# An encoder kernel on one core: the dt step cut into four pieces, the gates' products in 512 columns, the norm's second half on VectorE

## The chip, the core and the metric

One core of a Trainium2 chip runs the kernel. Five engines work on their own queues and wait for each other by semaphores: TensorE (PE, with its weight loads shown as PEld), VectorE (DVE), ScalarE (ACT), GpSimd (POOL) and SyncE (SP, which only issues transfers here). The metric is the device time of one execution in microseconds (us).

## The reference, cut to what matters

Two layers, 512 tokens of width 1024, all in float32. Each layer is

```
h    = rms_norm(x, norm1_w)
z, xbc, dt_raw, q, k, v = split(h @ w_in)
xs, B, C = split(silu(conv7(xbc)))
dt   = softplus(dt_raw + dt_bias)                  # two directions x 16 heads
y    = ssd(xs, dt, -exp(a_log), B, C) forward + backward + d_skip * xs
y    = rms_norm(y * silu(z))                       # per group of 512
attn = windowed_gqa(q, k, v, sink, bias)
x    = x + concat(y, attn) @ w_out
h    = rms_norm(x, norm2_w);  g, u = split(h @ w_up)
x    = x + (silu(conv3(g)) * u) @ w_down
```

and a final norm. The state-space part (ssd) works in chunks of 128 tokens: it needs the running sums of `a*dt` inside a chunk, their exponentials, and a decay matrix per head, `exp(sum_l - sum_s)`.

## The kernel before, in words

Tokens lie in four tiles of 128 (`NT`), the width in eight k-tiles. Every dense product is made of three matmuls (`mm3`, L277 to L280): each operand is split into a rounded part and a rest, and hi·hi, hi·lo and lo·hi are summed in PSUM. Weights come in units of 128 x 1024 by SP's DMA into three raw buffers; ACT rounds a unit (`whi`, L161), DVE makes the rest (`wlo`, L162), into three split buffers. `take` (L114) hands out a unit and issues the split of the unit three further on ahead of other work. PSUM has eight banks: four dense ones (`pd`, from `psd`) and four small ones (`psm`, from `pss`).

A scheduler sets the order of the instructions on each engine after `start.close()` (L538), from the order in the code and its own idea of when things are ready, so that a statement's place in the code isn't its place on an engine. Pools, buffer counts and priorities bind it.

The stages of a layer, in order: the value and dt columns (`vdt`); `dt_step` (L544), which makes softplus of dt in a chain of small DVE operations (`sp_e`, `sp_w`, `sp_a`), the running sums by six matmuls with triangular matrices (L581), their exponentials `ex` (L582), a logarithm of dt (`own`, L585 to L596), and turns the running sums `run` so that their transposes can go to DRAM (`sums`, L602), from where they are fetched as broadcast rows later; then the k columns; then ten dense pieces (list `dense`, L981), with attention's steps run in between (`Side`, L400); then the gates `g_z` (L832), with the steps of ssd group 0 in between: `fetch` (rows from DRAM), `decay` (L906 to L911: four additions and four exponentials on ACT, a predicated copy and a product `em` on DVE), `inner` (L922), `outer` (L937 to L945), and at the end a `turn` per token tile (L950); then the out projection `g_out` with ssd group 1 in between; `o2` and the norm; the FFN; `dn` and the next norm.

A gate unit is 4 k-tiles by 256 columns. A half of a group's columns takes two units, held together, and its four token tiles go in pairs: a pair fills one dense bank (2 x 256 columns, 48 matmuls), ACT takes Silu of the bank (L848), and ssd steps follow. Silu, Exp/Ln and the rest need different tables in ACT; the tables are loaded by ACT_TABLE_LOAD instructions in front of the operations that need them.

`norm_token` (L320) squares a token tile on ACT, finds the factor on POOL (L332, L333), and scales and weights both halves: the first by one DVE instruction (L342), the second by ACT (L344) and then POOL (L345). `turn_split` (L309) turns a half by four transposes, and ACT and DVE split it. It runs in three places: after `o2` of each layer and after `dn` of layer 0.

Of the kernel before, what the change touches and what calls it, by code (L numbers as in the profile page):

```python
# [7 lines left out]
F32 = mybir.dt.float32  # L8
# [38 lines left out]
def encoder_kernel(  # L47
# [122 lines left out]
    for i in range(DEPTH):  # L170
# [17 lines left out]
        for g in range(GROUPS):  # L188
            for half in range(2):
                pair(f"z{g}{half}", [(512 * g + 256 * half, 256)])  # L190
# [129 lines left out]
    def norm_token(npool, t, wb, dst):  # L320
# [13 lines left out]
        for b, cs in enumerate(halves):  # L334
            if dst is None:
                if b == 0:
                    S.mul(xn[:, cs], xn[:, cs], rs)
                else:
                    V.scalar_tensor_tensor(xn[:, cs], x_sb[t][:, cs], rs, wb[:, cs], ALU.mult, ALU.mult)
                nc.sync.dma_start(out[t * P : (t + 1) * P, cs], xn[:, cs])  # L340
            elif b == 0:
                V.scalar_tensor_tensor(xn[:, cs], x_sb[t][:, cs], rs, wb[:, cs], ALU.mult, ALU.mult)  # L342
            else:
                S.mul(xn[:, cs], x_sb[t][:, cs], rs)  # L344
                G.tensor_tensor(xn[:, cs], xn[:, cs], wb[:, cs], ALU.mult)  # L345
        if dst is None:
            return
        for b in range(2):
            turn_split(xn, t, b, dst)
# [120 lines left out]
    for i in range(DEPTH):  # L470
        side = Side()
        with ExitStack() as mix:
# [17 lines left out]
            dtx = ExitStack()  # L490
            dtp = dtx.enter_context(pool(f"dt_{i}", bufs=1, reuse_waits="tile"))
            run = dtp.tile([P, NT, 2, 16], F32, name=nm("run"))
            xdt = dtp.tile([P, NT, 32], F32, name=nm("xdt"))
# [49 lines left out]

            def dt_step():  # L544

                def et(name, shape, dt=F32):
                    return dtp.tile([P] + shape, dt, name=nm(name))

                sp_e = et("sp_e", [NT, 32])
                sp_w = et("sp_w", [NT, 32])  # L550
                sp_w2 = et("sp_w2", [NT, 32])
                sp_a = et("sp_a", [NT, 32])
# [7 lines left out]
                for n in (15, 13, 11, 9, 7, 5, 3):  # L560
# [4 lines left out]


                adt = sp_e
                V.scalar_tensor_tensor(
                    adt,
# [5 lines left out]
                )  # L575
                ps = small_bank()
                cum = ps[:, : 6 * 64].rearrange("p (n c h) -> p n c h", n=6, c=NT)
                for n, (m, o) in enumerate(
                    ((f(t_le), 0), (f(t_gt), 0), (f(t_ge), 16), (f(t_lt), 16), (ones, 0), (ones, 16))
                ):  # L580
                    mm(cum[:, n], m, adt[:, :, o : o + 16], start=True, stop=True)  # L581
                S.activation(ex, cum, AF.Exp)  # L582

# [6 lines left out]

                for d in range(2):
                    S.copy(run[:, :, d], cum[:, 2 * d])
# [4 lines left out]
                psr = small_bank()  # L597
                for c in range(NT):
                    turn128(psr[:32, c * P : (c + 1) * P], run[:, c].rearrange("p d h -> p (d h)"), ident)
                runT = dtp.tile([32, NT, P], F32, name=nm("runT"))  # L600
                V.tensor_copy(runT, psr[:32].rearrange("p (c l) -> p c l", c=NT))
                nc.gpsimd.dma_start(sums[i].rearrange("c r l -> r c l"), runT)  # L602
                V.tensor_tensor(sd[:, 0], ex[:, 1], dts[:, :, 0:16], ALU.mult)
                V.tensor_tensor(sd[:, 1], ex[:, 3], dts[:, :, 16:32], ALU.mult)
# [6 lines left out]
            dtx.close()  # L611
# [147 lines left out]
            def xbc(g, r):  # L759
# [16 lines left out]
                def bc_turn():  # L776
# [14 lines left out]
                    for c in range(NT):  # L791
                        sl = slice(c * P, (c + 1) * P)
                        junk = ep.tile([P, P], F32, tag="junk", name=nm("junk"), bufs=2)
# [38 lines left out]
            def g_z(g, r):  # L832
                sz = act_tile(F32)
                r["sz"] = sz
                for half in range(2):
                    ws = [take((i, f"z{g}{half}", j)) for j in range(2)]
                    cs = slice(256 * half, 256 * half + 256)
                    for tp in range(2):
                        bank = dense_bank()
                        for t in (2 * tp, 2 * tp + 1):  # L840
                            o = bank[:, (t % 2) * 256 : (t % 2) * 256 + 256]
                            sl = slice(t * P, (t + 1) * P)
                            for kt in range(KT):
                                hv, lv = (w.rearrange("p (k c) -> p k c", k=4)[:, kt % 4] for w in ws[kt // 4])
                                ah, al = hT[kt // 4]
                                mm3(o, ah[:, kt % 4, sl], al[:, kt % 4, sl], hv, lv, kt == 0, kt == KT - 1)
                        flush()
                        S.activation(sz[:, 2 * tp : 2 * tp + 2, cs], bank.rearrange("p (t c) -> p t c", t=2), AF.Silu)  # L848
                        yield
# [3 lines left out]
            def ssd_steps(sp, g, r):  # L853
# [123 lines left out]
                return [lambda k=k: step(k) for k in range(-1, 10)] + [lambda c=c: turn(c) for c in range(NT)]  # L977
# [3 lines left out]
            dense = [xs0[0], g_q(0), xs0[1], g_q(1), xs0[2], g_q(2), xs1[0], g_q(3), xs1[1], xs1[2]]  # L981
            for n, gen in enumerate(dense):
                side.run(gen, RATE_A if n > 1 else 0)
                if n == 7:
# [7 lines left out]
            side.steps += ssd_steps(sp, 0, r0)  # L992
# [10 lines left out]
            side.steps += ssd_steps(sp, 1, r1)  # L1003
# [151 lines left out]
```

## Time and profile before

| | |
|---|---|
| median of 3 runs | 1551.32 us (1548.27 to 1552.07) |
| the profiled execution | 1550.66 us, its span 1549.0 us |
| mean granted clock of TensorE | 0.994 of full speed |
| busy: PE, PEld, DVE | 1508.9, 1238.0, 876.5 us |
| busy: ACT, POOL | 793.4, 174.7 us |
| transfers | 161.48 MB, 104 GB/s over the span |

The span is the profiled stretch on the core; the execution's time also holds 1.66 us around it. PE is busy in nearly all of it, so the time is what PE has to do and the few places where it stands. Matmuls overlap, so an instruction's duration is longer than the distance to the next one: for sums, the distance between starts is used. Layer 0 begins at 0 us, layer 1 at 780 us; the gates of layer 0 run from 232 us to 306 us.

### The profile page before, as it was taken

How to read it: one execution, taken by the hardware profiler on the slowest of the kernel's cores; microseconds unless marked ns; L12 is line 12 of the kernel's file. 1: busy time of each engine (PE TensorE's matmuls, PEld its weight loads, DVE VectorE, ACT ScalarE, POOL GpSimd, SP SyncE). 2: the span in 40 equal slices, each digit the busy share in tenths (PEclk: the TensorE clock that was granted, in tenths of full speed). 3: DMA queues.
4: the chain of work that ended last, by engine and by line, in shares of the span. 5: the costliest groups of instructions: out<-in, count | busy, mean ns of one | idle time of the engine just before them, and what ended most of it. 6: DMA issues, size and time to landing. Idle time of an engine off the chain costs nothing.

```text
span 1549.0 us, 20219 instructions
## 1 busy us (share of the span) xinstructions
PE 1508.9 (97%) x7680; PEld 1238.0 (80%) x7680; DVE 876.5 (57%) x1406; ACT 793.4 (51%) x1464; POOL 174.7 (11%) x246
## 2 busy tenths in 40 slices
PE   7999999999999999999999999999999999999997
PEld 5787778877788888888887777887778888888886
DVE  5676777776644444433367777777666434443333
ACT  4467988863543233322356779788435323332223
POOL 2000002423200000000010000053232000000002
PEclk9899999999999999999999999999999999999999
DMA  6532333453323333322343322355422333333231
GB/s 206 156 82 76 83 85 103 134 169 95 108 88 98 102 95 96 95 96 95 99 137 104 89 75 62 83 123 182 132 95 82 95 97 101 101 96 96 95 96 68
DMA packets 113080, 161.48 MB, mean 104 GB/s; under 512 B 7932, under 2 KB 90108, under 8 KB 112975
## 3 DMA queue, kind: packets, MB, share of 16 engines
q1 hardware_dynamic: 104756, 132.60, 27.7%
q0 software_dynamic: 7648, 27.50, 6.7%
q8 instruction: 60, 0.98, 0.3%
q14 instruction: 38, 0.30, 0.1%
q10 hardware_dynamic: 578, 0.10, 0.0%
HBM read 155.82 MB, written 8.55 MB: 106 GB/s over the span
## 4 chain that ended last, share of the span: by engine, by line
PE 86%; ACT 4%; DVE 3%; issue 3%; POOL 2%; DMA 2%; POOLq 0%; ACTq 0%; DVEq 0%
PE pd L280 22%; PE pd L278 22%; PE pd L279 22%; PE psm L278 3%; PE psm L279 3%; PE psm L280 3%; PE psm L690 2%; PE psm L680 2%; PE psm L922 1%; PE psm L646 1%; DMA rows<-sums 1%; PE psm L647 1%; PE psm L937 1%; ACT whi L161 1%; PE psm L314 1%
## 5 line engine op out<-in xcount | busy, mean ns | idle before, releaser
L278 PE MATMUL pd<-t,whi 128*128 128x512 f32 (+1 forms) x1088 | 419.5, 386 | 1.5 <-ACT whi L161 1.5
L280 PE MATMUL pd<-t,wlo 128*128 128x512 f32 (+1 forms) x1088 | 419.4, 386 | 0.4 <-DVE wlo L162 0.4
L279 PE MATMUL pd<-t,whi 128*128 128x512 f32 (+1 forms) x1088 | 418.9, 385 | 0.0
L162 DVE TENSOR_TENSOR wlo<-raw,whi 128x1024 fp32r<-128x1024 f32 (+1 forms) x214 | 260.5, 1221 | 241.3 <-ACT whi L161 241.0
L161 ACT CAST whi<-raw 128x1024 fp32r<-128x1024 f32 (+1 forms) x214 | 221.8, 1040 | 240.9 <-PE pd L279 213.6
L278 PEld LDWEIGHTS pd<-t,whi 128*128 128x128 f32 x1088 | 204.7, 188 | 40.8 <-ACT whi L161 1.7
L280 PEld LDWEIGHTS pd<-t,wlo 128*128 128x128 f32 x1088 | 204.7, 188 | 40.2 <-issue 1.5
L279 PEld LDWEIGHTS pd<-t,whi 128*128 128x128 f32 x1088 | 205.0, 188 | 38.3 <-issue 0.8
L278 PE MATMUL pd<-whi,t 128*128 128x256 f32 (+2 forms) x544 | 188.9, 347 | 0.0
L279 PE MATMUL pd<-wlo,t 128*128 128x256 f32 (+2 forms) x544 | 180.3, 331 | 4.0 <-DVE wlo L162 3.9
L280 PE MATMUL pd<-whi,t 128*128 128x256 f32 (+2 forms) x544 | 181.7, 334 | 0.7 <-DVE t L962 0.7
L279 PEld LDWEIGHTS pd<-wlo,t 128*128 128x128 f32 x544 | 103.9, 191 | 17.2 <-DVE wlo L162 4.6
L278 PEld LDWEIGHTS pd<-whi,t 128*128 128x128 f32 x544 | 103.9, 191 | 13.7 <-issue 3.8
L280 PEld LDWEIGHTS pd<-whi,t 128*128 128x128 f32 x544 | 103.8, 191 | 11.5 <-DVE t L962 1.6
L1097 ACT CAST ph<-t 128x512 fp32r<-128x512 f32 x40 | 24.9, 623 | 143.0 <-PE psm L279 132.5
L1098 DVE TENSOR_TENSOR pl<-t,ph 128x512 fp32r<-128x512 f32 x40 | 27.7, 692 | 114.8 <-ACT ph L1097 114.8
L395 DVE SCALAR_TENSOR_TENSOR sg<-pd,fprm,sg 128x511 f32<-128x511 f32 x88 | 65.9, 748 | 30.7 <-ACT sg L389 29.0
L648 DVE CUSTOM_DVE_ANT_0 s<-psm,bias,sink_all 128x256 f32<-128x256 f32 (+1 forms) x128 | 65.6, 547 | 21.2 <-PE psm L647 8.0
L662 ACT ACTIVATE s<-s,nm 128x257 f32<-128x257 f32 (+1 forms) x128 | 70.5, 554 | 3.3 <-DVE nm L659 3.1
L395 DVE SCALAR_TENSOR_TENSOR xT<-pd,cprm,xT 128x511 f32<-128x511 f32 (+2 forms) x96 | 66.6, 742 | 5.2 <-PE psm L680 4.3
L278 PE MATMUL pd<-whi,ph 128*128 128x512 f32 x176 | 68.9, 391 | 0.0
L279 PE MATMUL pd<-wlo,ph 128*128 128x512 f32 x176 | 68.7, 390 | 0.0
(205 smaller groups left out, 2181.1 us busy)
## 6 DMA issues: line engine op xcount, KB each, us to landing
raw<-in_w_up_dram SPq DMA_DIRECT2D x88, 512.0 KB
raw<-in_w_in_dram SPq DMA_DIRECT2D x52, 512.0 KB
raw<-in_w_down_dram SPq DMA_DIRECT2D x44, 512.0 KB
rows<-sums POOLq DMA_DIRECT2D x32, 512.0 KB, 5.8
raw<-in_w_out_dram SPq DMA_DIRECT2D x32, 512.0 KB
bias<-toep POOLq DMA_DIRECT2D x16, 384.0 KB, 4.0
raw<-in_w_in_dram SPq DMA_DIRECT2D x18, 256.0 KB
x<-in_x_dram SPq DMA_DIRECT2D x8, 512.0 KB
```

What stands on the lines that cost most here:

```text
L161: S.copy(hi[:, :used], raw[:, :used])
L162: V.tensor_tensor(lo[:, :used], raw[:, :used], f(hi[:, :used]), ALU.subtract)
L278: mm(o, lh, rh, start=start, stop=False)
L279: mm(o, lh, rl, start=False, stop=False)
L280: mm(o, ll, rh, start=False, stop=stop)
L395: V.scalar_tensor_tensor(dst[:, lo:hi], src[:, lo + d : hi + d], taps[k], dst[:, lo:hi], ALU.mult, ALU.add)
L648: V.tensor_tensor_reduce(out=s4[:, h, :w], in0=ps[:, :w], in1=it.bias[h // 2][:, h % 2, it.j0 : it.j1], scale=1.0, scalar=sink4[:, h : h + 1],
L662: S.activation(s4[:, h, : w + 1], s4[:, h, : w + 1], AF.Exp, bias=nm4[:, h : h + 1], accum_out=den[:, h : h + 1])
L680: turn128(ps[:, c : c + P], it.s4[:, h, b * P : (b + 1) * P], ident)
L690: mm(po[c * HD : (c + 1) * HD, :256], v_sb[:, it.k0 // P + b, it.g * HD : (it.g + 1) * HD], it.pts[b][:, c * 256 : (c + 1) * 256], start=( ...
L1097: S.copy(h, p_sb[kt])
L1098: V.tensor_tensor(l, p_sb[kt], f(h), ALU.subtract)
```

## The change

A gate unit becomes 2 k-tiles by 512 columns. `g_z` takes all four dense banks, one per token tile, and goes over four units, each with 24 matmuls of 512 columns before ssd steps follow; the four Silus of a group (one per token tile) come in the last unit. The two units of a half were held together before; now one is held at a time.

`dt_step` keeps the softplus chain. The six matmuls, `ex`, `run` and `sd` become `dt_sums`, called after the second dense piece; the turns of `run` and their transfer become `dt_rows`, after the fourth; the logarithm and `own` become `dt_own`, after the sixth. Their tiles lie in the mixer's pool instead of a pool of their own, and `junk` has one buffer.

In `norm_token` both halves are scaled and weighted by DVE, and each is turned at once. `ssd_steps` returns its steps and its turns apart; the turns of group 0 stand behind the first step of group 1.

```diff
@@ -186,8 +186,8 @@
             else:
                 pair(nme, [(X0 + 512 * g + 256 * (nme[1] == "b"), 256)])
         for g in range(GROUPS):
-            for half in range(2):
-                pair(f"z{g}{half}", [(512 * g + 256 * half, 256)])
+            for j in range(4):
+                add_unit((i, f"z{g}", j), wi, 2 * j, 2, [(512 * g, 512)])
         for half in range(2):
             for j in range(6):
                 kt0 = (8 + 2 * j) if j < 4 else 2 * (j - 4)
@@ -338,15 +338,9 @@
                 else:
                     V.scalar_tensor_tensor(xn[:, cs], x_sb[t][:, cs], rs, wb[:, cs], ALU.mult, ALU.mult)
                 nc.sync.dma_start(out[t * P : (t + 1) * P, cs], xn[:, cs])
-            elif b == 0:
+            else:
                 V.scalar_tensor_tensor(xn[:, cs], x_sb[t][:, cs], rs, wb[:, cs], ALU.mult, ALU.mult)
-            else:
-                S.mul(xn[:, cs], x_sb[t][:, cs], rs)
-                G.tensor_tensor(xn[:, cs], xn[:, cs], wb[:, cs], ALU.mult)
-        if dst is None:
-            return
-        for b in range(2):
-            turn_split(xn, t, b, dst)
+                turn_split(xn, t, b, dst)
 
     def ws_part(key, j, acts, banks, w=None, sl=slice(0, L)):
 
@@ -487,10 +481,8 @@
             dts = ep.tile([P, NT, 32], F32, name=nm("dts"))
             ex = ep.tile([P, 6, NT, 16], F32, name=nm("ex"))
             sd = ep.tile([P, 2, NT, 16], F32, name=nm("sd"))
-            dtx = ExitStack()
-            dtp = dtx.enter_context(pool(f"dt_{i}", bufs=1, reuse_waits="tile"))
-            run = dtp.tile([P, NT, 2, 16], F32, name=nm("run"))
-            xdt = dtp.tile([P, NT, 32], F32, name=nm("xdt"))
+            run = ep.tile([P, NT, 2, 16], F32, name=nm("run"))
+            xdt = ep.tile([P, NT, 32], F32, name=nm("xdt"))
             vb = [dense_bank() for _ in range(NT)]
 
             def vdt(t, j):
@@ -541,15 +533,10 @@
                 for t, j in ((t, j) for t in range(NT) for j in range(3)):
                     vdt(t, j)
 
+            sp_e, sp_w, sp_w2, sp_a = (ep.tile([P, NT, 32], F32, name=nm("sp")) for _ in range(4))
+
             def dt_step():
 
-                def et(name, shape, dt=F32):
-                    return dtp.tile([P] + shape, dt, name=nm(name))
-
-                sp_e = et("sp_e", [NT, 32])
-                sp_w = et("sp_w", [NT, 32])
-                sp_w2 = et("sp_w2", [NT, 32])
-                sp_a = et("sp_a", [NT, 32])
                 V.scalar_tensor_tensor(sp_e, xdt, -1.0, xdt, ALU.mult, ALU.min)
                 S.activation(sp_e, sp_e, AF.Exp)
                 V.tensor_scalar(sp_w, sp_e, 2.0, None, ALU.add)
@@ -562,24 +549,39 @@
                 V.scalar_tensor_tensor(sp_a, sp_a, 1.0, sp_w, ALU.add, ALU.mult)
                 V.tensor_scalar(dts, xdt, 0.0, None, ALU.max)
                 V.scalar_tensor_tensor(dts, sp_a, 2.0, dts, ALU.mult, ALU.add)
-
-
-                adt = sp_e
                 V.scalar_tensor_tensor(
-                    adt,
+                    sp_e,
                     dts,
                     -1.0,
                     expa_all[:, 32 * i : 32 * i + 32].unsqueeze(1).broadcast_to([P, NT, 32]),
                     ALU.mult,
                     ALU.mult,
                 )
+
+            def dt_sums():
+
                 ps = small_bank()
                 cum = ps[:, : 6 * 64].rearrange("p (n c h) -> p n c h", n=6, c=NT)
                 for n, (m, o) in enumerate(
                     ((f(t_le), 0), (f(t_gt), 0), (f(t_ge), 16), (f(t_lt), 16), (ones, 0), (ones, 16))
                 ):
-                    mm(cum[:, n], m, adt[:, :, o : o + 16], start=True, stop=True)
+                    mm(cum[:, n], m, sp_e[:, :, o : o + 16], start=True, stop=True)
                 S.activation(ex, cum, AF.Exp)
+                for d in range(2):
+                    S.copy(run[:, :, d], cum[:, 2 * d])
+                V.tensor_tensor(sd[:, 0], ex[:, 1], dts[:, :, 0:16], ALU.mult)
+                V.tensor_tensor(sd[:, 1], ex[:, 3], dts[:, :, 16:32], ALU.mult)
+
+            def dt_rows():
+
+                psr = small_bank()
+                for c in range(NT):
+                    turn128(psr[:32, c * P : (c + 1) * P], run[:, c].rearrange("p d h -> p (d h)"), ident)
+                runT = ep.tile([32, NT, P], F32, name=nm("runT"))
+                V.tensor_copy(runT, psr[:32].rearrange("p (c l) -> p c l", c=NT))
+                nc.gpsimd.dma_start(sums[i].rearrange("c r l -> r c l"), runT)
+
+            def dt_own():
 
 
                 V.tensor_scalar(sp_w, dts, 1e-37, None, ALU.max)
@@ -587,28 +589,16 @@
                 S.activation(sp_w2, sp_a, AF.Exp, scale=-1.0)
                 V.tensor_tensor(sp_w, sp_w, sp_w2, ALU.mult)
                 V.scalar_tensor_tensor(sp_a, sp_w, -1.0, sp_a, ALU.add, ALU.add)
-
-                for d in range(2):
-                    S.copy(run[:, :, d], cum[:, 2 * d])
                 V.tensor_tensor(
                     own.rearrange("p c d h -> p c (d h)"), sp_a, run.rearrange("p c d h -> p c (d h)"), ALU.subtract
                 )
                 V.tensor_tensor(own[:, :, 1], own[:, :, 1], own[:, :, 0], ALU.subtract)
-                psr = small_bank()
-                for c in range(NT):
-                    turn128(psr[:32, c * P : (c + 1) * P], run[:, c].rearrange("p d h -> p (d h)"), ident)
-                runT = dtp.tile([32, NT, P], F32, name=nm("runT"))
-                V.tensor_copy(runT, psr[:32].rearrange("p (c l) -> p c l", c=NT))
-                nc.gpsimd.dma_start(sums[i].rearrange("c r l -> r c l"), runT)
-                V.tensor_tensor(sd[:, 0], ex[:, 1], dts[:, :, 0:16], ALU.mult)
-                V.tensor_tensor(sd[:, 1], ex[:, 3], dts[:, :, 16:32], ALU.mult)
 
             if i == 0:
                 setup()
                 setupx.close()
                 first.close()
             dt_step()
-            dtx.close()
 
 
             mixA = []
@@ -790,7 +780,7 @@
                     own_cb = smp.tile([P, NT], F32, tag="own_cb", name=nm("own_cb"))
                     for c in range(NT):
                         sl = slice(c * P, (c + 1) * P)
-                        junk = ep.tile([P, P], F32, tag="junk", name=nm("junk"), bufs=2)
+                        junk = ep.tile([P, P], F32, tag="junk", name=nm("junk"), bufs=1)
                         V.scalar_tensor_tensor(
                             junk, ps[:, sl], 1.0, ident, ALU.mult, ALU.mult, accum_out=own_cb[:, c : c + 1]
                         )
@@ -832,21 +822,21 @@
             def g_z(g, r):
                 sz = act_tile(F32)
                 r["sz"] = sz
-                for half in range(2):
-                    ws = [take((i, f"z{g}{half}", j)) for j in range(2)]
-                    cs = slice(256 * half, 256 * half + 256)
-                    for tp in range(2):
-                        bank = dense_bank()
-                        for t in (2 * tp, 2 * tp + 1):
-                            o = bank[:, (t % 2) * 256 : (t % 2) * 256 + 256]
-                            sl = slice(t * P, (t + 1) * P)
-                            for kt in range(KT):
-                                hv, lv = (w.rearrange("p (k c) -> p k c", k=4)[:, kt % 4] for w in ws[kt // 4])
-                                ah, al = hT[kt // 4]
-                                mm3(o, ah[:, kt % 4, sl], al[:, kt % 4, sl], hv, lv, kt == 0, kt == KT - 1)
-                        flush()
-                        S.activation(sz[:, 2 * tp : 2 * tp + 2, cs], bank.rearrange("p (t c) -> p t c", t=2), AF.Silu)
-                        yield
+                banks = [dense_bank() for _ in range(NT)]
+                for j in range(4):
+                    hi, lo = take((i, f"z{g}", j))
+                    hv = hi.rearrange("p (k c) -> p k c", k=2)
+                    lv = lo.rearrange("p (k c) -> p k c", k=2)
+                    for t in range(NT):
+                        sl = slice(t * P, (t + 1) * P)
+                        for k in range(2):
+                            kt = 2 * j + k
+                            ah, al = hT[kt // 4]
+                            mm3(banks[t], ah[:, kt % 4, sl], al[:, kt % 4, sl], hv[:, k], lv[:, k], kt == 0, kt == KT - 1)
+                        if j == 3:
+                            S.activation(sz[:, t], banks[t], AF.Silu)
+                    flush()
+                    yield
 
             mixS = [None, None]
 
@@ -974,13 +964,16 @@
                     if odd and c in range(NT):
                         outer(c)
 
-                return [lambda k=k: step(k) for k in range(-1, 10)] + [lambda c=c: turn(c) for c in range(NT)]
+                return [lambda k=k: step(k) for k in range(-1, 10)], [lambda c=c: turn(c) for c in range(NT)]
 
             r0, r1 = {}, {}
             xs0, xs1 = xbc(0, r0), xbc(1, r1)
             dense = [xs0[0], g_q(0), xs0[1], g_q(1), xs0[2], g_q(2), xs1[0], g_q(3), xs1[1], xs1[2]]
+            later = {1: dt_sums, 3: dt_rows, 5: dt_own}
             for n, gen in enumerate(dense):
                 side.run(gen, RATE_A if n > 1 else 0)
+                if n in later:
+                    later[n]()
                 if n == 7:
                     side.steps += [lambda: attn_push(None)] * (LAG + 1)
             flush()
@@ -989,7 +982,8 @@
 
             spx = ExitStack()
             sp = spx.enter_context(pool(f"ssd_{i}", bufs=1, reuse_waits="tile"))
-            side.steps += ssd_steps(sp, 0, r0)
+            steps0, turns0 = ssd_steps(sp, 0, r0)
+            side.steps += steps0
             side.run(g_z(0, r0), RATE_S)
             side.run(g_z(1, r1), RATE_S)
             mixT = []
@@ -1000,7 +994,8 @@
                     S.copy(h[:, k], a)
                     V.tensor_tensor(l[:, k], a, f(h[:, k]), ALU.subtract)
                 mixT.append((h, l))
-            side.steps += ssd_steps(sp, 1, r1)
+            steps1, turns1 = ssd_steps(sp, 1, r1)
+            side.steps += steps1[:1] + turns0 + steps1[1:] + turns1
 
 
             x_sb = load_x(x_in if i == 0 else x_dram)
```

What the scheduler makes of it is seen in three places. In the changed kernel L568 is the running sums' matmul (L581 before), L579 the turn of `run` (L599), L896 and L899 decay's additions and exponentials (L906, L909), L837 the gates' Silu (L848), L935 the square in `outer` (L945), L994 the split of attention's output `x` (L1000).

PE in layer 1, around the running sums (`sp_e` or `sp`), before; `pd` are the banks of the piece bc0:

```order
L279 MATMUL pd_7440<-t_1355_6462,whi_3740 128x512
L581 MATMUL psm_7341<-sp_e_7319,t_le 128x64
L581 MATMUL psm_7341<-sp_e_7319,t_gt 128x64
L581 MATMUL psm_7341<-sp_e_7319,t_ge 128x64
L581 MATMUL psm_7341<-sp_e_7319,t_lt 128x64
L581 MATMUL psm_7341<-sp_e_7319,ones 128x64 x2
L280 MATMUL pd_7440<-t_1354_6461,wlo_3741 128x512
L278 MATMUL pd_7441<-t_1354_6461,whi_3740 128x512
L279 MATMUL pd_7441<-t_1355_6462,whi_3740 128x512
L280 MATMUL pd_7441<-t_1354_6461,wlo_3741 128x512
L599 MATMUL psm_7358<-ident,run_7209 32x128 x4
L278 MATMUL pd_7441<-t_1354_6461,whi_3740 128x512
```

and now:

```order
L279 MATMUL pd_7274<-t_1357_6264,whi_3557 128x512
L280 MATMUL pd_7274<-t_1356_6263,wlo_3558 128x512
L568 MATMUL psm_7340<-sp_7112,t_le 128x64
L568 MATMUL psm_7340<-sp_7112,t_gt 128x64
L568 MATMUL psm_7340<-sp_7112,t_ge 128x64
L568 MATMUL psm_7340<-sp_7112,t_lt 128x64
L568 MATMUL psm_7340<-sp_7112,ones 128x64 x2
L278 MATMUL pd_7352<-t_1354_6261,whi_3563 128x512
L279 MATMUL pd_7352<-t_1355_6262,whi_3563 128x512
L280 MATMUL pd_7352<-t_1354_6261,wlo_3564 128x512
L278 MATMUL pd_7352<-t_1354_6261,whi_3563 128x512
```

The sums' matmuls stood inside bc0, with the four turns of `run` four matmuls behind them; now they stand two pieces later, between the last matmul of q0 and the first of xa0, and the turns are not near them.

PE in layer 0, the same place, before:

```order
L581 MATMUL psm_481<-sp_e_459,t_ge 128x64
L581 MATMUL psm_481<-sp_e_459,t_lt 128x64
L581 MATMUL psm_481<-sp_e_459,ones 128x64 x2
L278 MATMUL pd_514<-t_10_121,whi_516 128x512
L599 MATMUL psm_498<-ident,run_185 32x128 x4
L279 MATMUL pd_514<-t_11_122,whi_516 128x512
L278 MATMUL pd_515<-t_10_121,whi_516 128x512
```

and now:

```order
L568 MATMUL psm_732<-sp_406,t_ge 128x64
L568 MATMUL psm_732<-sp_406,t_lt 128x64
L568 MATMUL psm_732<-sp_406,ones 128x64 x2
L278 MATMUL pd_483<-t_10_121,whi_485 128x512
L279 MATMUL pd_483<-t_11_122,whi_485 128x512
L278 MATMUL pd_484<-t_10_121,whi_485 128x512
L279 MATMUL pd_484<-t_11_122,whi_485 128x512
```

Here the sums' matmuls stay in front of the first matmul of the k columns; only the turns of `run` have left.

ACT at the end of layer 0's gates, before; `rows` are decay's rows, the last `pd` is a gate bank, `whi` a weight unit, and the CASTs of L1000 split attention's output for the out projection:

```order
L909 ACT_TABLE_LOAD
L909 ACTIVATE rows_2827<-rows_2827,own_178 128x128 x3
L909 ACTIVATE rows_2914<-rows_2914,own_178 128x128 x3
L945 ACTIVATE y_3009,gss_3023<-t_470_2414 128x512
L909 ACTIVATE rows_2914<-rows_2914,own_178 128x128
L1000 CAST t_570_3114<-x_102_757 128x512 x2
L161 CAST whi_2938<-raw_2775 128x1024
L1000 CAST t_570_3114<-x_169_1054 128x512
L161 CAST whi_3146<-raw_2936 128x1024
L848 ACT_TABLE_LOAD
L848 ACTIVATE t_523_2764<-pd_3045 128x2x256
L1000 CAST t_570_3114<-x_169_1054 128x512
```

and now:

```order
L837 ACT_TABLE_LOAD
L837 ACTIVATE t_523_2664<-pd_2665 128x512
L899 ACT_TABLE_LOAD
L899 ACTIVATE rows_2766<-rows_2766,own_178 128x128
L935 ACTIVATE y_2829,gss_2843<-t_470_2410 128x512
L161 CAST whi_2950<-raw_2788 128x1024
L899 ACTIVATE rows_2766<-rows_2766,own_178 128x128 x3
L837 ACT_TABLE_LOAD
L837 ACTIVATE t_523_2664<-pd_2666 128x512
L837 ACTIVATE t_523_2664<-pd_2667 128x512
L837 ACTIVATE t_523_2664<-pd_2668 128x512
L994 CAST t_570_2918<-x_99_726 128x512 x2
```

The first split of attention's output stood ahead of the last Silu, and stands now behind all four Silus of the last unit and two table loads between them.

## Rows read from the trace of the kernel before

**Rows 1.** The page, part 1: busy us (share of the span), instructions.
```profile
PE 1508.9 (97%) x7680; PEld 1238.0 (80%) x7680; DVE 876.5 (57%) x1406; ACT 793.4 (51%) x1464; POOL 174.7 (11%) x246
```
**Rows 2.** Stretch by engine: us, PE, PEld, DVE, ACT, POOL busy, clock, DMA, GB/s.
```profile
248.00:340.00 92.00, 88.04 (x535) 74.58 (x535) 66.27 (x81) 77.17 (x168) 32.21 (x35) 1.00 0.56 155
```
**Rows 3.** Groups by line and form: count, busy us, mean ns, idle before.
```profile
L278 PE MATMUL pd<-whi,t 128*128 128x256 f32 x256 | 74.8, 292 | 0.0
```
**Rows 4.** Timeline of PE, steady stretches: start, duration, tiles, [idle before <-releaser].
```profile
301.40 0.28 PE L278 MATMUL pd<-whi,t 128*128 128x256 f32 x1
...
303.44 0.28 PE L280 MATMUL pd<-whi,t 128*128 128x256 f32 x1
...
812.18 0.39 PE L278 MATMUL pd<-t,whi 128*128 128x512 f32 x1
...
813.77 0.39 PE L279 MATMUL pd<-t,whi 128*128 128x512 f32 x1
```
**Rows 5.** Timeline of PE, waits in the gates of both layers.
```profile
286.17 0.38 PE L278 MATMUL pd<-whi,t 128*128 128x256 f32 x1
288.51 0.39 PE L279 MATMUL pd<-wlo,t 128*128 128x256 f32 x1 [1.95 <-DVE wlo L162]
...
300.28 1.10 PE L922 MATMUL psm<-t,em 128*128 128x64 f32 x8 [1.25 <-DVE em L911]
...
1047.02 0.39 PE L279 MATMUL pd<-wlo,t 128*128 128x256 f32 x1 [1.95 <-DVE wlo L162]
```
**Rows 6.** Timeline of ACT and DVE before the wait at 288.51.
```profile
286.33 1.03 ACT L161 CAST whi<-raw 128x1024 fp32r<-128x1024 f32 x1
...
287.23 2.35 DVE L162 TENSOR_TENSOR wlo<-raw,whi 128x1024 fp32r<-128x1024 f32 x2
```
**Rows 7.** The gates' Silu line: count, duration min/median/max in ns, first and last start.
```profile
L848 ACT ACTIVATE t<-pd x16: 590/598/601, 240.4 to 1064.7; 128x512 f32<-128x512 f32 x16
L848 ACT ACT_TABLE_LOAD  x14: 1283/1283/1283, 237.6 to 1063.4; - x14
```
**Rows 8.** Timeline at the end of layer 0's gates: ACT, DVE, PE.
```profile
300.64 1.12 ACT L1000 CAST t<-x 128x512 fp32r<-128x512 f32 x2
...
304.87 1.28 ACT L848 ACT_TABLE_LOAD   x1
306.16 0.60 ACT L848 ACTIVATE t<-pd 128x512 f32<-128x512 f32 x1
...
306.00 0.68 DVE L1001 TENSOR_TENSOR t<-x,t 128x512 fp32r<-128x512 f32 x1
...
304.40 1.08 PE L937 MATMUL psm<-st,cT 128*128 128x512 f32 x2
```
**Rows 9.** Timeline of PE, layer 0's dt step.
```profile
39.76 0.66 PE L581 MATMUL psm<-sp_e,t_le 128*128 128x64 f32 x2 [4.89 <-DVE sp_w L585]
...
44.06 0.79 PE L278 MATMUL pd<-t,whi 128*128 128x512 f32 x1 [1.51 <-ACT whi L161]
```
**Rows 10.** Timeline of PE and ACT, layer 1's dt step.
```profile
814.67 0.43 PE L581 MATMUL psm<-sp_e,t_le 128*128 128x64 f32 x2 [0.51 <-DVE sp_e L568]
...
818.86 0.61 PE L599 MATMUL psm<-ident,run 128*32 128x128 f32 x4 [1.66 <-ACT run L592]
...
816.61 1.28 ACT L587 ACT_TABLE_LOAD   x1
```
**Rows 11.** Timeline of PE and DVE at the norm after o2, layer 0.
```profile
426.13 0.65 PE L314 MATMUL psm<-ident,xn 128*128 128x128 f32 x4 [0.59 <-POOL xn L345]
...
417.82 3.76 DVE L162 TENSOR_TENSOR wlo<-raw,whi 128x1024 fp32r<-128x1024 f32 x3 [0.34 <-ACT whi L161]
...
424.01 0.75 DVE L342 SCALAR_TENSOR_TENSOR xn<-x,rs,wb 128x512 f32<-128x512 f32 x1 [0.63 <-POOL rs L333]
```
**Rows 12.** Layer 0's gates: ACT waiting for a transfer; the page, part 6, that transfer.
```profile
281.41 0.99 ACT L906 ACTIVATE rows<-rows,own 128x128 f32<-128x128 f32 x3 [2.39 <-DMA rows<-sums]
...
rows<-sums POOLq DMA_DIRECT2D x32, 512.0 KB, 5.8
```

## The prediction

> **What bounds the kernel now.** I read the engines' busy times first, then the stretches, then where PE stands. PE is busy for 1508.9 us of the 1549.0 us span, no other engine for more than 57% [rows 1]. So the time is PE's work, plus its waits, and an edit pays only where it shortens one of the two. The gates and the first part of the out projection show the gap best: in the 92 us from 248 us PE is busy for 88.04, and ACT for 77.17, more than its 51% over the span [rows 2]. ACT is the engine that PE meets there.
>
> **Gates in 512 columns.** The gates are 768 matmuls of 256 columns; one of the three lines shows 256 of them [rows 3]. Their starts are 2.04 us apart over 17 intervals, 0.120 us each, and matmuls of 512 columns are 1.59 us apart over 7, 0.227 us each [rows 4]. So 768 x 0.120 = 92.2 us becomes 384 x 0.227 = 87.2 us: 5.0 us less over both layers, 2.5 each. The durations (292 ns for 256 columns) overlap and would mislead here.
>
> The Trainium skill, page "TensorE: Matmul & The Clock Gate", section "Back-to-back issue gap", gives an isolated gap of N/2.4 plus about 2.5 ns. By that the gap is 109 and 216 ns, an estimate from the page, and this edit saves only 1.0 us. The trace has 120 and 227 ns in steady stretches of this very kernel, and it decides.
>
> A unit wait goes. In the middle of the second group PE starts a half at 286.17 and its second matmul at 288.51: 2.34 us where 0.12 is due, so 2.2 lost [rows 5]. The half holds two units; DVE reaches its `wlo` only at 287.23, behind ACT's cast at 286.33 [rows 6]. Layer 1 has the same wait at 1047.02 [rows 5]. With one unit held at a time, the split of the next stands 24 matmuls, 5.4 us, ahead. I take 2.2 per layer; bounds 0 (the wait moves to another unit) and 2.2.
>
> At 300.28 PE waits 1.25 us for `em` [rows 5]. This one hangs on ACT's exponentials; the gates' Silus come in with table loads of 1283 ns, 14 of them in both layers [rows 7], and the new order has 8. I take 0.5 us per layer, between 0 and 1.8 (that wait and a smaller one).
>
> What comes in its place is the head of the out projection. All four banks are now held until the last unit, and the out projection needs them for its first product. Before, the first casts of attention's output ran at 300.64, well ahead of the last Silu at 306.16 [rows 8]; in the new order they stand behind everything. After the last gate matmul ACT has a cast of a unit (1.03 [rows 6]), three exponentials (the three additions at 281.41 took 0.99 [rows 12]), a table load (1.28 [rows 7]), three Silus (3 x 0.60, some overlap, so 1.6 [rows 7]) and a cast (1.12 for two, 0.56), then DVE the rest (0.68) [rows 8]: 1.0 + 1.0 + 1.3 + 1.6 + 0.6 + 0.7 = 6.2 us, and I take 6.0. PE has meanwhile eight inner products (1.10 busy [rows 5]), the outer ones (1.08 [rows 8]) and three turns of four transposes that stood later (0.65 each [rows 11]): 4.1 us busy, overlapping, so some 3.0 us. New wait: 3.0 us per layer. Bounds: 0, where ACT is early by then, and 6.0, where PE's other work waits too.
>
> A second price: the last attention items' transposes now stand in front of the gates, where they stood behind thirteen gate matmuls, so PE meets the scaled scores early. No row shows that wait; the nearest is the wait for `em` of 1.25 us [rows 5]. I take 1.0 per layer, bounds 0 and 1.25.
>
> Per layer: -2.5 - 2.2 - 0.5 + 3.0 + 1.0 = -1.2; both layers -2.4.
>
> **The dt step.** The order shows that layer 0 hardly gets what the edit's words say: sums, exponentials and logarithm stay ahead of the k columns, and only the turns of `run` leave. PE's wait of 4.89 us at 39.76 and that of 1.51 at 44.06 for the first unit of k both stay, since both their causes do [rows 9]. The turns that leave cost PE what they take, but come back later; DVE's copy and the transfer no longer stand in the way of k. I take -0.5, bounds 0 and -1.8 (the wait at 44.06 gone).
>
> In layer 1 both waits go. Before, PE stood 0.51 us for the softplus chain and 1.66 us for `run`, whose copy on ACT stood behind table loads such as that at 816.61 [rows 10]. The first is 0.90 between starts, 813.77 to 814.67, where 0.23 is due [rows 4, 10], so 0.67 lost; the second in the same way 1.83; together 2.5 us. Now the sums stand between q0 and xa0, some 20 us behind the chain, and the turns stand in a later piece among attention. One more table load comes for `ex`, 1.28 us of ACT between two of q0's scalings; xa0's matmuls take other banks, so it is hidden; without that cover it costs 1.3. I take -2.5, bounds -2.5 and -1.2.
>
> The transfer of `sums` now stands on POOL between bias transfers and the copies that attention's scores need. POOL is busy for 174.7 us in the span [rows 1]. But it waits for `runT` there, and with it POOL's next copy, and PE for that. I take 0, bounds -1 and +1.
>
> **The norms.** Three places of the same form. PE waits 0.59 us for POOL's product [rows 11], some 0.75 with what it loses around the wait, as above. The second half now runs on DVE behind the first, in 0.75 us [rows 11], so it is there before the first half's turns end. The first half's wait stays. Against it, DVE takes 0.67 us more per token, and at 417.82 it has three `wlo` in a row [rows 11], so that the last token's addition comes 0.3 us later. Net -0.5 at each, -1.5 in all; bounds 0 and -2.3.
>
> **The sum.** -2.4 - 0.5 - 2.5 - 1.5 = -6.9 us, from 1550.66 us (span 1549.0 and 1.66 around it) to 1543.8 us. That execution is 0.66 us below the median of 1551.32, so the median comes to 1544.4 us.
>
> **Rivals.**
> *A, all of it kept.* The two prices (the head, the transposes) turn out as nothing, because fewer table loads bring ACT there early: -6.9 - 2 x 4.0 = -14.9, 1536.4 us. For it: six table loads of the gates are gone, 6 x 1.283 = 7.7 us of ACT [rows 7]. Against it: up to the first cast ACT has one more Silu and two more unit casts in the new order, about as much work. The Trainium skill, page "ScalarE: Activation LUTs", section "What ACT_TABLE_LOAD costs", adds a drain of about 1380 ns to each load; by it the gain on ACT would be twice as large, and A likelier. No drain is seen in the trace: at 304.87 a load starts and at 306.16 the Silu, 1.29 us later [rows 8].
>
> *B, given back.* PE's side work at the head waits for the same ACT chain, so that the whole 6.0 us are idle: 2 x 3.0 more, -0.9, 1550.4 us. For it: inner products wait for `em`, which waits for exponentials that stand behind a Silu and two table loads. Against it: the turns of the first group don't.
>
> *C, slower.* ACT works in order, and three exponentials that need rows from DRAM stand in front of three of the Silus that free the banks. At 281.41 ACT stood 2.39 us for such rows, and they take 5.8 us from issue to landing [rows 12]. If the fetch of the last unit comes so late that PE sees the landing and the chain to the first exponential (from 281.41 [rows 12] to the cast at 286.33 [rows 6], 4.9, about 5 us), 5.8 + 5.0 - 3.0 = 7.8 us more are lost per layer: -6.9 + 15.6 = +8.7, 1560.0 us. It decides from 5.8 us more per layer, where the sum reaches +4.65. Against it: three row buffers, so fetches run a unit or two ahead.
>
> **How the numbers follow.** Main case 0.42 (1540 to 1548 by its own bounds), A 0.22, B 0.22, C 0.14. A measurement of this kernel tells 0.3%, 4.65 us, from no change: below 1546.7 is faster, above 1556.0 slower. Of the main case 0.04 lies above 1546.7, so faster is 0.38 + 0.22 = 0.60, the same 0.04 + 0.22 = 0.26, slower 0.14. The range goes from A's 1536.4, with 1 us for its own spread, to B's with 4 us towards C: 1535 to 1555, which leaves out C and the lower tail of A.
>
> **What would show it.** Right: gate matmuls 0.227 us apart and no wait for `wlo` inside the gates; layer 1 without waits at its running sums; one wait instead of two per norm; at the head of each out projection a wait of about 3 us for ACT's cast or Silu. Layer 0's 4.89 us still there. Wrong: the wait at the head absent (A) or over 5 us (B, and C if it names rows), the dt wait of layer 0 gone, or a wait for POOL in attention behind the transfer of `sums`.

## The result, and the profile after

The changed kernel took 1567.36 us (median of 4 runs, 1565.86 to 1568.03), the kernel before 1551.69 us beside it: 15.7 us slower, ratio 1.0099 with a 95% interval of 1.0083 to 1.0115. The forecast was 1544.4 us in 1535 to 1555, faster.

The page of the changed kernel, its span, part 1, and the granted clock in 40 slices:

```profile
span 1564.2 us, 19394 instructions
...
PE 1516.5 (97%) x7296; PEld 1223.1 (78%) x7296; DVE 879.3 (56%) x1418; ACT 776.3 (50%) x1444; POOL 166.6 (11%) x234
...
PEclk9899999899999999999999999998999999999999
```

The same clock line of the kernel before:

```profile
PEclk9899999999999999999999999999999999999999
```

PE has 384 matmuls fewer and is busy 7.6 us longer than in [rows 1]: work that is fewer but longer points to the clock, and the clock line has two new dips. Cutting both traces where stages begin (by the starts of the first dense matmul of each) puts the loss in three lines:

| us, layer 0 / layer 1 | before | changed |
|---|---|---|
| first to last gate matmul | 71.60 / 71.53 | 64.43 / 64.44 |
| from there to the first of the out projection | 1.47 / 1.47 | 9.94 / 9.59 |
| first half of the out projection | 39.83 / 40.36 | 45.42 / 46.83 |

The gates are 7.2 and 7.1 us shorter, part of it because 12 of attention's last 20 value products (L690) and 8 transposes of scores now stand ahead of them; what follows is 14.1 and 14.6 us longer. PE at the head of layer 0's out projection, then the granted clock there (columns as in [rows 2]):

```profile
298.36 0.39 PE L280 MATMUL pd<-whi,t 128*128 128x512 f32 x1
298.59 1.02 PE L927 MATMUL psm<-st,cT 128*128 128x512 f32 x2
299.44 1.04 PE L949 MATMUL psm<-ident,t 128*128 128x128 f32 x8
303.77 1.11 PE L949 MATMUL psm<-ident,t 128*128 128x128 f32 x4 [3.29 <-DVE yo L929]
306.57 1.97 PE L912 MATMUL psm<-t,em 128*128 128x64 f32 x8 [1.69 <-DVE em L901]
308.30 0.77 PE L278 MATMUL pd<-whi,t 128*128 128x512 f32 x1
308.87 0.63 PE L279 MATMUL pd<-wlo,t 128*128 128x512 f32 x1
309.30 0.63 PE L278 MATMUL pd<-whi,t 128*128 128x512 f32 x1
```
```profile
300.00:305.00 5.00, 1.59 (x9) 0.95 (x7) 2.37 (x4) 4.97 (x11) 2.96 (x4) 0.85 0.00 0
305.00:310.00 5.00, 3.43 (x12) 2.87 (x12) 2.83 (x4) 1.40 (x3) 1.74 (x2) 0.50 0.53 161
310.00:315.00 5.00, 4.63 (x14) 3.42 (x13) 4.84 (x8) 4.84 (x11) 2.36 (x3) 0.62 0.63 161
```

Three turns and the inner products now stand in front of the out projection and wait themselves. After 3.3 us of idling the clock is at its lower level, 1.2 GHz: matmuls start 0.43 us apart (308.87, 309.30) where [rows 4] has 0.227. ACT in the same time, and the two steps on DVE that hold the third turn:

```profile
296.45 1.28 ACT L837 ACT_TABLE_LOAD   x1
297.74 0.60 ACT L837 ACTIVATE t<-pd 128x512 f32<-128x512 f32 x1
298.36 1.28 ACT L899 ACT_TABLE_LOAD   x1
...
299.96 0.61 ACT L935 ACTIVATE y<-t 128x512 f32<-128x512 f32 x1
...
300.58 1.03 ACT L161 CAST whi<-raw 128x1024 fp32r<-128x1024 f32 x1
301.51 0.98 ACT L899 ACTIVATE rows<-rows,own 128x128 f32<-128x128 f32 x3
302.51 1.28 ACT L837 ACT_TABLE_LOAD   x1
303.80 1.57 ACT L837 ACTIVATE t<-pd 128x512 f32<-128x512 f32 x3
305.25 1.15 ACT L994 CAST t<-x 128x512 fp32r<-128x512 f32 x2
```
```profile
302.63 0.49 DVE L945 TENSOR_SCALAR t<-t,rs 128x512 f32<-128x512 f32 x1 [3.50 <-POOL rs L289]
303.03 0.68 DVE L929 TENSOR_TENSOR yo<-psm,ex 128x512 f32<-128x512 f32 x1
...
304.76 1.75 DVE L901 TENSOR_TENSOR em<-rows,cb 128x512 f32<-128x512 f32 x1
```

ACT is busy without a gap. The casts of attention's output begin at 305.25, 6.9 us behind the last gate matmul; before they ran 2.8 us ahead of it (300.64 [rows 8]). DVE stands at L945 for a factor from POOL, which waited for the square on ACT (299.96), which stood behind Silu and the second table load; `yo`, queued behind L945, empties the small bank that PE names. The first Silu was through at 298.34, so the first of the four dense banks was free ten us before the first product of the out projection: that product doesn't wait for a bank. The description of the kernel is too coarse on tables: a load stands between Ln and Exp as well (816.61 [rows 10]), while a cast follows Silus without one (305.25).

The second stop of layer 0, PE and then ACT:

```profile
333.16 0.60 PE L949 MATMUL psm<-ident,t 128*128 128x128 f32 x4
...
340.26 0.50 PE L278 MATMUL pd<-whi,t 128*128 128x512 f32 x1 [2.40 <-ACT t L951]
340.60 0.39 PE L279 MATMUL pd<-wlo,t 128*128 128x512 f32 x1
341.64 0.80 PE L280 MATMUL pd<-whi,t 128*128 128x512 f32 x1 [0.65 <-DVE t L952]
342.23 0.63 PE L278 MATMUL pd<-whi,t 128*128 128x512 f32 x1
342.66 0.63 PE L279 MATMUL pd<-wlo,t 128*128 128x512 f32 x1
```
```profile
337.22 0.40 ACT L896 ACTIVATE rows<-rows,own 128x128 f32<-128x128 f32 x1 [3.41 <-DMA rows<-sums]
...
339.63 0.57 ACT L951 CAST t<-psm 128x512 fp32r<-128x512 f32 x1
```

The last token's turn was ready to be split at about 333.8, but its cast waits in ACT's queue behind an addition of group 1 that waits 3.41 us for rows from DRAM. The last units of this half need that token. Then the clock falls again (342.23 and 342.66 are 0.43 apart).

What was forecast to go did go: the running sums of layer 1 no longer stop PE, and a norm has one wait where [rows 11] belongs to two:

```profile
840.71 0.33 PE L568 MATMUL psm<-sp,t_le 128*128 128x64 f32 x2
```
```profile
433.63 0.63 PE L314 MATMUL psm<-ident,xn 128*128 128x128 f32 x4 [0.49 <-DVE xn L342]
...
434.33 0.60 PE L314 MATMUL psm<-ident,xn 128*128 128x128 f32 x4
```

### The profile page after: what moved, and what is told of

It reads as the page before. It is cut to its first block, busy times and chain, and to the rows that moved or that the text cites. A ratio compares the mean times of both kernels' runs of the same rounds, so it can differ in the third digit from the quotient of the medians.

```text
span 1564.2 us, 19394 instructions
## 1 busy us (share of the span) xinstructions
PE 1516.5 (97%) x7296; PEld 1223.1 (78%) x7296; DVE 879.3 (56%) x1418; ACT 776.3 (50%) x1444; POOL 166.6 (11%) x234
## 4 chain that ended last, share of the span: by engine, by line
PE 82%; DVE 5%; issue 4%; DMA 4%; ACT 3%; POOL 2%; POOLq 0%; SPq 0%; ACTq 0%; DVEq 0%
PE pd L280 20%; PE pd L278 20%; PE pd L279 20%; DMA rows<-sums 3%; PE psm L278 3%; PE psm L279 3%; PE psm L280 3%; PE psm L680 2%; PE psm L670 2%; PE psm L636 1%; PE psm L912 1%; PE psm L870 1%; PE psm L637 1%; DVE wlo L162 1%; PE psm L927 1%
## 5 line engine op out<-in xcount | busy, mean ns | idle before, releaser
L278 PE MATMUL pd<-whi,t 128*128 128x512 f32 (+1 forms) x416 | 171.0, 411 | 4.9 <-ACT t L951 4.8
L280 PE MATMUL pd<-whi,t 128*128 128x512 f32 (+1 forms) x416 | 160.2, 386 | 2.0 <-DVE t L952 1.3
L279 PE MATMUL pd<-wlo,t 128*128 128x512 f32 (+1 forms) x416 | 158.9, 382 | 0.1
L278 PEld LDWEIGHTS pd<-whi,t 128*128 128x128 f32 x416 | 80.2, 193 | 25.5 <-ACT t L951 6.9
L280 PEld LDWEIGHTS pd<-whi,t 128*128 128x128 f32 x416 | 79.9, 192 | 19.3 <-DVE t L952 2.7
L279 PEld LDWEIGHTS pd<-wlo,t 128*128 128x128 f32 x416 | 80.1, 193 | 18.3 <-issue 5.1
L389 DVE SCALAR_TENSOR_TENSOR xT<-pd,cprm,xT 128x509 f32<-128x509 f32 (+2 forms) x96 | 67.5, 743 | 3.3 <-ACT xT L383 3.2
```

The costliest lines, as they stand in the source:

```text
L278: mm(o, lh, rh, start=start, stop=False)
L279: mm(o, lh, rl, start=False, stop=False)
L280: mm(o, ll, rh, start=False, stop=stop)
L389: V.scalar_tensor_tensor(dst[:, lo:hi], src[:, lo + d : hi + d], taps[k], dst[:, lo:hi], ALU.mult, ALU.add)
```

## Experiments

The median of the kernel before, over all runs beside these, was 1551.6 us (1546.67 to 1554.37).

**One part alone, and all but one.** The first has the kernel before with the new gate units and loop; the second has the changed kernel with the old ones.

```diff
# gates alone: the kernel before, and only
-                pair(f"z{g}{half}", [(512 * g + 256 * half, 256)])
+                add_unit((i, f"z{g}", j), wi, 2 * j, 2, [(512 * g, 512)])
# and g_z as in the change; all but the gates: the reverse, on the changed kernel
```

> The kernel before with the gate units of 2 k-tiles x 512 columns and nothing else. Theory H (the gates make the loss: after the last gate matmul PE waits for the Silu and exponential chain, 5.4 us a layer, and then runs at the 1.2 GHz level; the moved turns add the second stop in the out projection, about 5 us a layer): 1551.7 + 10 to 12 us, about 1562 us, with the head as in the changed kernel (9 to 10 us from the last gate matmul to the first of the out projection) and no stop at the last token's turn. Rival T (the order of the turns alone makes the loss): 1546 to 1551 us. Rival D (the dt pieces make it): 1546 to 1551 us.

> The changed kernel with the old gate units and the old gate loop; dt pieces, norm and turn order stay. Theory H: no loss is left, 1551.7 - 2.5 (layer 1's dt waits) - 2.4 (norms) - 0.5 = about 1546 us, if the late turn does not meet a late chain here; up to 1556 us if the moved turns stop the out projection by themselves. Rival T: 1560 us or more. Rival D: 1560 us or more.

Gates alone: 1560.63 us, ratio 1.0057 (1.0042 to 1.0072); the head is 9.84 and 9.82 us as in the changed kernel, the second stop is absent. So the gates lose 9.0 us by themselves, a little less than the 10 to 12 of theory H. All but the gates: 1552.42 us, ratio 1.0006 (0.9994 to 1.0019), between H's two figures; its ten runs spread from 1549.52 to 1557.56, and the profiled one took 1556.66. Its head is as before, but the stop at the last token is there; PE, then ACT:

```profile
334.89 0.50 PE L278 MATMUL pd<-whi,t 128*128 128x512 f32 x1 [2.00 <-ACT t L951]
```
```profile
332.73 0.69 ACT L896 ACTIVATE rows<-rows,own 128x128 f32<-128x128 f32 x2 [0.54 <-DMA rows<-sums]
333.32 1.03 ACT L161 CAST whi<-raw 128x1024 fp32r<-128x1024 f32 x1
334.26 0.57 ACT L951 CAST t<-psm 128x512 fp32r<-128x512 f32 x1
```

The turn order makes that stop with either gates. The wait for rows is not always the larger part of it: in the changed kernel 3.41 of the 5.9 us between the turn's end and its cast are that wait, here 0.8 of 5.5, and the rest is group 1's additions and exponentials and a unit's cast, which stand in front as well.

**The place of the turns.**

```diff
-            side.steps += steps0
+            side.steps += steps0 + turns0
...
-            side.steps += steps1[:1] + turns0 + steps1[1:] + turns1
+            side.steps += steps1 + turns1
```

> The changed kernel with group 0's turns issued straight after its steps, as before. Theory H: the second stop (PE 2.6 and 0.8 us for the last token's split, then 1.2 GHz for some microseconds) goes, the head stays: 1567.4 - 2 x 5 = about 1557 us. Rival T: about 1545 us. If the place of the turns does nothing: 1567 us.

1556.19 us, ratio 1.0032 (1.002 to 1.0044): 11.2 us of the loss go, as H had it (10), and the second stop with them; the first half of the out projection takes 40.51 and 39.67 us. The head stays at 9.76 and 9.79 us. T, which has the turns as the whole cause, falls.

**The splits of attention's output earlier.** The first half of them is issued after the third unit of group 1's gates, the second half stays behind the gates.

```diff
+                    if j == 2 and early:
+                        early()
...
+            side.run(g_z(1, r1, lambda: mix_split(0)), RATE_S)
+            mix_split(1)
```

> The changed kernel with the first half of attention's output split inside group 1's gates, after its third unit, instead of behind its last Silu. Theory H (PE stands at the head for turns and for em, which hang on Silu and exponentials, not on these casts): head shorter by 1 to 2 us a layer at most, 1563 to 1567 us. Rival C (the casts behind the Silus are what the head waits for, as my prediction priced it): 5 us a layer and more gone, 1557 us or less.

1559.33 us, ratio 1.0045 (1.003 to 1.006): 8.0 us gained, twice what H allowed and short of the 10 of this run's rival C (not the C of the prediction). PE at the head, then ACT:

```profile
301.42 0.39 PE L280 MATMUL pd<-whi,t 128*128 128x512 f32 x1
301.65 1.02 PE L929 MATMUL psm<-st,cT 128*128 128x512 f32 x2
302.10 0.80 PE L278 MATMUL pd<-whi,t 128*128 128x512 f32 x1
...
307.01 1.10 PE L914 MATMUL psm<-t,em 128*128 128x64 f32 x8 [1.57 <-DVE em L903]
```
```profile
304.51 1.58 ACT L837 ACTIVATE t<-pd 128x512 f32<-128x512 f32 x3
```

With the operand ready, the scheduler puts twelve products of the out projection in front of the inner products, and the turns behind them. They can only be in the first bank, which the first Silu had freed: the other Silus begin at 304.51. So the late casts matter in two ways: nothing else can run, and the order is filled with turns that wait. The run moves both together and can't tell how much is either. H as put on record is wrong here: it took the turns in front for given.

**Both of these.** The two edits in one kernel.

> The changed kernel with both: group 0's turns straight after its steps (11.2 us gained alone) and the early splits (8.0 us gained alone). If the two losses are separate places that add up: 1567.4 - 11.2 - 8.0 = about 1548 us. If they share the half-clock time or the same chain, 1552 to 1556 us.

1544.34 us, ratio 0.9957 (0.994 to 0.9973): 23 us less than the changed kernel, more than the 19.2 of the two alone, and faster than the kernel before. From the first gate matmul to the first of `o2` the profiles nearly add up: over both layers the changed kernel's stretch gets 12.2 us shorter by the turns, 10.7 by the splits and 21.6 by both. The rest lies outside: in layer 1's attention PE waits 2.57 and 2.43 us for DVE's step on the scores (`m`) in the two runs with one edit, 1.36 in the changed kernel and 1.98 here, and no run shows why. The head is down to 0.68 us; what is left is a wait for `em` behind it:

```profile
303.53 0.40 PE L278 MATMUL pd<-whi,t 128*128 128x512 f32 x1
305.52 0.66 PE L914 MATMUL psm<-t,em 128*128 128x64 f32 x4 [1.59 <-DVE em L903]
```

**The dt pieces and the norm alone,** with old gates and old turns (the edit of the turns on the kernel that has all but the gates).

> The kernel before with the dt pieces and the norm alone (old gates, old place of the turns). My terms for these, -0.5 - 2.5 - 1.5, and 0.8 more for the norms as the trace of the changed kernel has them: 1546 to 1547 us. If the moved turns are the 5 us a layer that the run without the gates lost, 1552.4 - 10 = 1542.5 us. If the dt pieces cost anything by themselves: 1550 us or more.

1545.87 us, ratio 0.9971 (0.9957 to 0.9984): 5.7 us gained, where my terms had 4.5 to 5.3. The second figure, 1542.5, was too low: with the old gates the turns cost 1552.42 - 1545.87 = some 6.6 us, not 10.

**Silu late.** Old turns; group 1's banks are emptied by copies, which need no table.

```diff
+                            if g:
+                                S.copy(sz[:, t], banks[t])
...
+            late = [lambda t=t: S.activation(r1["sz"][:, t], r1["sz"][:, t], AF.Silu) for t in range(NT)]
+            side.steps += steps1[:2] + [lambda: [k() for k in late]] + steps1[2:] + turns1
```

> The changed kernel with the old place of the turns, and group 1's four gate banks drained by plain copies on ACT (no table), their Silu done in place during the out projection. Theory H (PE stands at the head for what is queued on ACT behind Silu and its two table loads): the head's 5.3 us of waits fall below 2.5 us and the 1.2 GHz stretch goes, 1556.2 - 2 x 5 = about 1546 us. Rival R (the wait at the head is for the banks or for POOL and DVE, whatever ACT does): within 2 us of 1556.

1549.57 us, ratio 0.9992 (0.9981 to 1.0003): 6.6 us less than with the old turns alone. The head has one wait left:

```profile
299.64 1.10 PE L915 MATMUL psm<-t,em 128*128 128x64 f32 x8 [1.05 <-DVE em L904]
300.58 1.08 PE L930 MATMUL psm<-st,cT 128*128 128x512 f32 x2
301.10 0.79 PE L278 MATMUL pd<-whi,t 128*128 128x512 f32 x1
301.73 0.39 PE L279 MATMUL pd<-wlo,t 128*128 128x512 f32 x1
```
```profile
298.26 0.61 ACT L997 CAST t<-x 128x512 fp32r<-128x512 f32 x1
```

The first cast comes at 298.26, with the old turns alone at 304.63, because neither Silus nor tables stand in front. The copies also empty the banks earlier, so this run alone doesn't part casts and banks; but the early splits, with the Silus as they were, let the first product start 0.68 us behind the last gate matmul. Rival R, which had no gain, falls. The size was missed by 3.6 us. From the first gate matmul to the first of `o2` this run is 7.2 and 3.8 us shorter than with the old turns alone (in layer 1 PE stands 2.47 us for ACT's copy of a state, L877, and is granted 0.66 of full clock in the 5 us from 1097), and from there to the first of `dn` 3.3 and 3.2 us longer: of group 1's four turns only two are through before `o2`, and in layer 0 the norm's transposes wait 1.7 us for DVE in three places, against 0.5 in one.

**Late Silu and early splits.**

> The same as the one before it, with the early splits besides. Theory H: the first product of the out projection then waits for nothing on ACT, 1 to 4 us better than it, about 1543 us. Rival (the casts only take ACT's time from the exponentials inside the gates): no better, or 1 to 3 us worse.

1544.86 us, ratio 0.9968 (0.9953 to 0.9983): 4.7 us better than without the splits, and level with the 1544.34 of splits and turns alone. H's direction holds. Beside splits and turns it is 4.2 and 2.9 us shorter from the first gate matmul to the first of `o2`, and gives back 3.4 us a layer from there to `dn`, for group 1's late turns and the norm's waits.

## Why the prediction was wrong, step by step

- **Gates in 512 columns, the unit wait: right.** No `wlo` wait is left inside the gates. Beside the run with dt and norm alone, which has the same side work in its gates, they go from 68.42 and 69.98 us, first to last gate matmul, to 64.43 and 64.44: 4.0 and 5.5 us less, where 2.5 + 2.2 + 0.5 = 5.2 was forecast. The 0.5 for `em` did not come: in layer 0 PE loses 1.06, 0.56 and 0.66 us to it.
- **The head of the out projection: the step that failed.** The prediction named the place and the chain, casts behind four Silus, and priced it at 6.0 us of ACT against "some 3.0 us" of PE's own work, so 3.0 us. The distance from the last gate matmul to the first of the out projection is 9.94 us instead of 1.47. ACT's chain was summed from the last gate matmul on, but ACT then still had a table load, an exponential and the square in front, and came to the unit's cast, the first item of the sum, 2.2 us later (300.58); from there to attention's first cast it took 4.7 us, where the sum has 4.9. The PE work put against the chain was itself hung on it: the third turn waits 3.29 us, the inner products 1.69, so PE stands 5.0 us. Rival B had that half of it, though it left out the turns. And no term had the clock: after the idling, 24 products of the out projection took 8.53 us, 0.6 of it a wait; at full clock they take 5.87 (all but the gates), or 6.23 with a turn among them, as before. The inner products took 1.73 us from their start to the next instruction's instead of 0.84. So the loss at this place is 8.5 and 8.1 us at the head and 2.3 and 2.1 behind, less 0.8 for two turns that would have come later: 10.0 and 9.4 us in the two layers, against 3.0.
- **The turns of the first group: not in the sum at all.** The change puts them behind a step of group 1, and the prediction counted them only as work that PE has at the head. They cost 11.2 us over both layers with the new gates and 6.6 with the old. The mechanism is near rival C's, a piece of ACT's queue behind additions that wait for rows from DRAM (and behind the exponentials that follow them), at a place that the prediction didn't look at: its own price for C was for the Silus.
- **Attention's transposes ahead of the gates, +1.0 a layer: wrong.** They moved, but with dt and norm alone the dense pieces are 3.32 us longer and the gates 3.18 shorter in layer 0, so they cost next to nothing; and they move with the dt pieces, not with the gates: with the gates alone all 20 value products stay among the gates, with dt and norm alone 8 do.
- **dt and norms: right.** Layer 0's first wait stays (4.50 us, 4.89 before), layer 1's two are gone, a norm saves some 0.8 us in the changed kernel and 0.6 with dt and norm alone, where 0.5 was taken; together 5.7 us measured, 4.5 forecast.

The parts add up: +9.0 (gates alone), -5.7 (dt and norms), +11.2 (turns, taken out last) make +14.5 of the 15.7 us. What stays open is the share of the lower clock: no run held the clock up through the same idling, so its cost is known from the distances only, at layer 0's head some 3 us (2.1 in the 24 products, 0.9 in the inner ones). Nor was it tried to move the turns behind the out projection's first unit without moving the casts.

## What to carry to other kernels

A stretch without waits on the busy engine can be shortened at a loss if the work that joins it to the next stretch hangs on an engine that works in order: ask when that engine gets to the first operand of the next stage, here a cast behind Silus and table loads, and put the cast ahead. Work counted as cover for a chain must be checked for hanging on the same chain. When small steps are put in another order, ask of each what it stands behind on the helpers' queues, and for which transfers from DRAM that queue waits.

## What the hardware showed that was not expected

The lower clock level came after a short idling: PE stood 3.3 us, had done 1.6 us of work in 5, and the next 10 us were granted 0.50 to 0.62 of full speed. The same followed the waits of 2.4 and 0.65 us at 340.26 and 341.64 (the granted clock of the 5 us around them):

```profile
340.00:345.00 5.00, 4.10 (x9) 2.52 (x10) 2.22 (x3) 3.42 (x9) 0.00 (x0) 0.66 0.31 105
```

The wait of 2.2 us in the gates before [rows 5] had left the clock at 1.00 [rows 2]. So a wait can cost more than its own time, at the head some 3 us in the matmuls at and behind it. The length of the wait alone doesn't tell whether it does. In the run with both edits PE waits 1.59 us for `em` in each layer; behind the first the clock falls, behind the second it stays (PE's wait in layer 1, then the 5 us behind each):

```profile
1062.05 1.10 PE L914 MATMUL psm<-t,em 128*128 128x64 f32 x8 [1.59 <-DVE em L903]
```
```profile
305.00:310.00 5.00, 4.48 (x18) 3.77 (x19) 3.70 (x7) 2.88 (x8) 1.61 (x3) 0.72 0.63 180
1065.00:1070.00 5.00, 5.00 (x24) 4.13 (x23) 5.00 (x8) 5.00 (x14) 2.67 (x3) 1.00 0.82 197
```
